# Part norms summed before their ones-product, a projection block moved ahead of an attention block, 1/rms on token quarters, lo parts on GpSimd

## The chip, the cores and the metric

The kernel runs on one core of a Trainium2 chip. The metric is the device time of one execution in microseconds (us), as the median of several runs. Nothing but the kernel runs on the chip at that time.

## What is computed

One Hymba-style decoder block on 512 tokens of width 1024, all in f32. Cut to what matters here:

```python
mod = silu(c) @ ada_w + ada_b                     # shift, scale, gate, twice
h = modulate(rmsnorm(x, norm1_g), shift1, scale1)
q, k, v, cb, cc, cu = split(h @ w_in)             # 18 blocks of 128 columns
attn = sliding_window_attention(q, k, v, sinks)   # window 128, 8 heads of 64
conv = cb * short_conv(cc * cu, conv_w)           # causal, width 3
merged = concat(rmsnorm(attn, g_a), rmsnorm(conv, g_c))   # the part norms
x = x + gate1 * (merged @ w_out)
h2 = modulate(rmsnorm(x, norm2_g), shift2, scale2)        # the second norm
x = x + gate2 * peer(h2, wq, subkeys, u_tab, v_tab)       # 16384 experts, top 16 per head
```

## The kernel before

Activations lie transposed: 128 partitions of columns by 512 tokens, so a norm over columns is a sum over partitions, made on TensorE by a product with a matrix of ones. A weight block (`raw`, 128x1024) is loaded by an SP DMA into one of five buffers. `split` (L175 to L177) makes of it `hi` on ScalarE (ACT, L176) and `lo = raw - hi` on VectorE (DVE, L177), and `mm3` (L197) issues 24 matmuls for it: L200 hi by H, L201 hi by L, and L202 lo by H.

Ahead of the experts there is a front part of some 260 us, and the change lies there. After the first norm come the projection blocks (`proj`, L336; four of the 18 are made earlier), mixed with the attention. The string `PLAN` (L50) sets the order in which they are written: `C m part` is a projection block of the short convolution (`conv`, L437), where part 0 ends in a copy `cc` on ACT, part 1 in `hb` and `y` on DVE and part 2 in `convT` on DVE. `A n` is `attend1` (L373) for query block n: eight score products `sc`, their scaling `s` on DVE (L388), the maximum `m` (L391), its negative `nm` (L394), eight exponentials on ACT (L397), and a division on DVE (L405). `B n` is `attend2` (L408): each head's `s` is transposed on TensorE (`pT`, L416), copied out by ACT (L418) and multiplied with the values (`po`, L425). `M` is two columns' blocks of the modulation matrix (`junk`, L213, on DVE). `S` is the sum of squares of the convolution part (`ssc`), and `N` makes its normed parts `mH`, `mL` (`part_norm`, L463).

After the plan comes `ssa`, the sum of squares of the attention part (L518 to L520). `square` (L234) squares one 128x512 slice on ACT and issues a ones-product for it, so each part norm has four products. `rstd` (L239) takes the root on ACT and the reciprocal on DVE, on 128x512, where all 128 partitions hold the same row. Then come the output products `py` (`out_half`, L472): first the half that needs the convolution part, for four blocks, then the other half and the other blocks. The residual `xT` is squared block by block and summed on DVE, and two ones-products (L551, L552) give `ss2`. `spill` (L528) transposes `xT` back to token rows (`xt`), copies it out on ACT (`xn`, L535, three buffers) and stores it. `modulated` (L226) makes `f`, `fH`, `fL` of the second norm, which the queries (`pq`) and their scores (`psc`, L742) take, ACT's copies `qs` (L735) between them. Everything behind that (keys, sorting, dense experts, gathered rows) the change leaves alone.

A scheduler fixes each engine's order of instructions when the kernel is built; on the chip every engine works through its own in that order and waits on semaphores. PSUM has six rotating banks (`bank`) and two for accumulators (`psa`).

Of the kernel before, what the change touches and what calls it, by code (L numbers as in the profile page):

```python
# [7 lines left out]
F32 = mybir.dt.float32  # L8
# [10 lines left out]
P = 128  # L19
T = 512  # L20
# [26 lines left out]

PLAN = ("q0 q1 k P2 M r0 V R P3 r1 q2 C00 r2 q3 T C01 M r3 M C02 A0 C10 M C11 A1 M C12 B0 C20 M M M A2 C21 B1 A3 "  # L50
        "C30 M C22 C31 C32 S B2 N B3 M M M")

SM = {}
# [36 lines left out]
def body(tc, p):  # L90
# [13 lines left out]
    rt, rt_s = pool("rt", side="right")  # L104
    R2 = dict(tag="s2", bufs=3)
    tp, tp_s = pool("tp", side="right")
    T2 = dict(tag="t2", bufs=9)
    xp, xp_s = pool("xp", side="right")

    def bank(name):  # L110
# [10 lines left out]
    def S(n, i=None, w=1):  # L121
        a, b = SM[n]
        return sm[:, a:b] if i is None else sm[:, a + i:a + i + w]
# [48 lines left out]
            tc.add_manual_dep(ins.ins, mark.ins.name, mybir.DependencyInfo(  # L172
                mybir.DependencyClass.Sync, mybir.DependencyReason.DATA), reason="pace")

    def split(h, l, f):  # L175
        nc.scalar.activation(h, f, AF.Copy)  # L176
        nc.vector.tensor_sub(l, f, h.bitcast(F32))  # L177

    def load(src):
        raw = ld.tile([P, D], F32, tag="ld", bufs=LD, name="raw")  # L180
        nc.sync.dma_start(raw, src)
        return raw

    def parts(src):

        raw = load(src)
        h = hl.tile([P, D], F32R, tag="h", bufs=4, name="hi")
        l = hl.tile([P, D], F32R, tag="l", bufs=4, name="lo")
        split(h, l, raw)
        return h, l  # L190

    def weights_of(src):

        h, l = parts(src.rearrange("p a b -> p (a b)"))
        return (lambda k: h[:, k * P:(k + 1) * P]), (lambda k: l[:, k * P:(k + 1) * P])

    def mm3(ps, w, rh, rl, ks=range(DC), k0=0, k1=DC - 1):  # L197
# [36 lines left out]
    def square(ps, b, i, n, w=None):  # L234
        q = tmp("sq")
        nc.scalar.activation(q, b, AF.Square)
        nc.tensor.matmul(ps, ones if w is None else w, q, start=(i == 0), stop=(i == n - 1))

    def rstd(ps, n):  # L239
        r = tmp("rstd")  # L240
# [93 lines left out]
    attnT = a1.tile([P, 4, T], F32, name="attnT")  # L334

    def proj(b):  # L336
        w = weights_of(p["w_in"][b])
        ps = bank("pj")
        mm3(ps, w, hh, hlo)
        return ps  # L340
# [119 lines left out]
    vT = tmp("vT")  # L460
    nc.scalar.activation(vT, pj[5], AF.Copy)
    kg = S("kg")
    def part_norm(ss, src, g, o):  # L463
        r = rstd(ss, 512)
        for k in range(4):
            f = tmp("f")
            nc.vector.scalar_tensor_tensor(f, src[:, k, :], S(g, k), r, op0=OP.mult, op1=OP.mult)
            split(mH[:, o + k, :], mL[:, o + k, :], f)
# [12 lines left out]
    for step in PLAN.split():  # L481
        n = [int(x) for x in step[1:]]
        match step[0]:
            case "k":
                nk = qk1(pj[4], qk0(pj[4]), kg)
            case "q":
                nq[n[0]] = q0(pj[n[0]], n[0])
            case "P":
                pj[n[0]] = proj(n[0])
            case "V":  # L490
                pt = bank("vt")
                for c in range(NCH):
                    nc.tensor.transpose(pt[:, c * P:(c + 1) * P], vT[:, c * P:(c + 1) * P], ident)
                nc.scalar.activation(vN.rearrange("p a b -> p (a b)"), pt, AF.Copy)
            case "r":
                qk2(nq.pop(n[0]), qT[:, n[0], :])
            case "R":
                qk2(nk, kT)
            case "T":
                nc.scalar.activation(rq, ssq, AF.Sqrt, bias=eps64)  # L500
                nc.vector.reciprocal(rq, rq)
            case "A":
                sa[n[0]] = attend1(n[0])
            case "B":
                attend2(n[0], sa[n[0]])
            case "C":
                conv(*n)
            case "M":
                more_ada()
            case "S":  # L510
                ssc = bank("ssc")
                for k in range(4):
                    square(ssc, convT[:, k, :], k, 4)
            case "N":
                mH = a1.tile([P, DC, T], F32R, tag="hH", name="mH")
                mL = a1.tile([P, DC, T], F32R, tag="hL", name="mL")
                part_norm(ssc, convT, "cg", 0)
    ssa = bank("ssa")  # L518
    for k in range(4):
        square(ssa, attnT[:, k, :], k, 4)  # L520
    for b in range(HEAD):
        out_half(b, 0)
    part_norm(ssa, attnT, "ag", 4)
    ab = S("ada_b")
# [3 lines left out]
    def spill(half, when):  # L528
        for c in range(NCH):
            ps = bank("xt")  # L530
            for i in range(4):
                after(nc.tensor.transpose(ps[:, i * P:(i + 1) * P], xT[:, 4 * half + i, c * P:(c + 1) * P], ident),
                      when)
            xn = rt.tile([P, 512], F32, name="xn", **R2)
            nc.scalar.activation(xn, ps, AF.Copy)  # L535
            nc.sync.dma_start(x1s[c][:, half * 512:(half + 1) * 512], xn)

# [10 lines left out]
        if b < 6:  # L548
            more_ada(3)
    sq = squared(xT[:, 6, :], sq)  # L550
    nc.tensor.matmul(ss2, ones, sq, start=True, stop=False)  # L551
    end = nc.tensor.matmul(ss2, ones, squared(xT[:, 7, :]), start=False, stop=True)  # L552
    nc.vector.tensor_add(mod[:, 24:48], mod[:, 24:48], ab[:, 24:48])
    nc.vector.scalar_tensor_tensor(s2, mod[:, 32:40], 1.0, S("n2g"), op0=OP.add, op1=OP.mult)
    a1_s.close()
# [16 lines left out]
    hx, hx_s = pool("hx")  # L572
    fH = hx.tile([P, DC, T], F32R, name="fH")
    fL = hx.tile([P, DC, T], F32R, name="fL")
    r2 = rstd(ss2, D)
    spill(0, end)
    spill(1, end)
    early = [(weights_of(p["wq"][b]), bank("pq")) for b in range(EARLY)]
    fs = []
# [552 lines left out]
```

## Time and profile before

| what | value |
|---|---|
| median of 3 runs | 1447.48 us (1445.46 to 1451.26) |
| profiled execution, own time | 1445.51 us |
| its span, first to last instruction | 1443.6 us |
| mean granted TensorE clock | 0.989 |
| busy: PE, DVE, ACT, POOL | 1391.7, 1242.0, 616.1, 411.4 us |

PE is TensorE, ACT ScalarE, POOL GpSimd, SP the engine that issues loads. Lines named L... are lines of the kernel before. The granted clock is a share of 2.4 GHz.

### The profile page before, as it was taken

The page shows a single profiled execution, that of the slowest core. Times are in us where ns is not written, and L with a number is a line of the kernel's source. Part 1 is how long each engine was busy: PE and PEld are TensorE (multiplying, and loading weights), DVE is VectorE, ACT ScalarE, POOL GpSimd, SP SyncE. Part 2 cuts the span into 40 slices and gives each one's busy share as a digit, 9 for nine tenths or more (in the row PEclk, how much of TensorE's full clock was granted, in tenths as well). Part 3 has the DMA queues.
Part 4 walks back from the last instruction along what each step waited for, and adds up shares of the span by engine and source line. Part 5 has one row for each costly group of instructions (what it writes and reads, how often), then busy time and mean ns, then how long its engine had stood idle before and what let it go on. Part 6 is the DMA issues. An engine that isn't in the chain of part 4 may idle for free.

```text
span 1443.6 us, 21238 instructions
## 1 busy us (share of the span) xinstructions
PE 1391.7 (96%) x7696; PEld 1222.1 (85%) x7696; DVE 1242.0 (86%) x2267; ACT 616.1 (43%) x1041; POOL 411.4 (29%) x292
## 2 busy tenths in 40 slices
PE   6999998999897999999999999999999999999998
PEld 4776776788897999999888888889999999889997
DVE  7778978799989999998668888888789988898964
ACT  4534646423633555464433434343343324333431
POOL 0000000000032330511034444446545546565400
PEclk9999999999998999999999999999999999999999
DMA  8645535222496997898999999999999999999843
GB/s 282 226 164 166 202 124 188 82 85 89 151 305 200 382 377 280 327 384 325 364 332 362 409 395 378 396 357 380 355 362 394 388 357 343 363 343 393 319 146 131
DMA packets 134377, 418.80 MB, mean 290 GB/s; under 512 B 12801, under 2 KB 39553, under 8 KB 132737
## 3 DMA queue, kind: packets, MB, share of 16 engines
q1 hardware_dynamic: 92800, 266.45, 51.1%
q0 software_dynamic: 41472, 151.01, 27.7%
q8 instruction: 60, 0.98, 0.3%
q14 instruction: 45, 0.36, 0.1%
HBM read 375.77 MB, written 41.62 MB: 289 GB/s over the span
## 4 chain that ended last, share of the span: by engine, by line
PE 63%; DVE 24%; DMA 5%; issue 5%; ACT 2%; POOL 1%; SPq 0%; DVEq 0%; ACTq 0%; POOLq 0%
PE o L997 11%; PE o L996 11%; PE o L998 11%; PE pa L200 6%; PE pa L202 6%; PE pa L201 6%; DVE lo L177 4%; DVE junk L213 2%; DVE B L946 2%; DVE junk L784 1%; PE py L200 1%; PE py L201 1%; DVE I L636 1%; PE py L202 1%; POOL row L776 1%
## 5 line engine op out<-in xcount | busy, mean ns | idle before, releaser
L176 ACT ACTIVATE hi<-raw 128x1024 fp32r<-128x1024 f32 x298 | 312.2, 1054 | 308.2 <-PE pa L201 71.7
L177 DVE TENSOR_TENSOR lo<-raw,hi 128x1024 fp32r<-128x1024 f32 x298 | 363.2, 1221 | 42.4 <-ACT hi L176 42.0
L202 PE MATMUL pa<-h2H,lo 128*128 128x352 f32 x1024 | 330.5, 323 | 8.2 <-DVE lo L177 8.2
L200 PE MATMUL pa<-h2H,hi 128*128 128x352 f32 x1024 | 332.9, 325 | 1.4 <-ACT sp L624 1.4
L201 PE MATMUL pa<-h2L,hi 128*128 128x352 f32 x1024 | 329.5, 322 | 0.0
L997 PE MATMUL o<-lo,wwh 128*128 128x512 f32 x768 | 299.2, 390 | 0.9 <-DVE lo L177 0.9
L996 PE MATMUL o<-hi,wwh 128*128 128x512 f32 x768 | 299.6, 390 | 0.0
L998 PE MATMUL o<-hi,wwl 128*128 128x512 f32 x768 | 298.8, 389 | 0.0
L776 POOL DMA_INDIRECT row<-in_uR,eG x128 | 187.4, 1464 | 319.5 <-PE o L998 181.8
L776 POOL DMA_INDIRECT row<-in_vL,eG x128 | 179.8, 1405 | 135.4 <-PE o L998 68.6
L784 DVE SCALAR_TENSOR_TENSOR junk<-row,h2N 128x1024 bf16<-128x1024 f32 x128 | 154.2, 1224 | 63.0 <-DMA row<-in_uR,eG 62.8
L202 PEld LDWEIGHTS pa<-h2H,lo 128*128 128x128 f32 x1024 | 193.2, 189 | 9.4 <-DVE lo L177 9.4
L200 PEld LDWEIGHTS pa<-h2H,hi 128*128 128x128 f32 x1024 | 192.7, 188 | 3.7 <-ACT sp L624 1.5
L201 PEld LDWEIGHTS pa<-h2L,hi 128*128 128x128 f32 x1024 | 193.1, 189 | 2.2
L912 DVE SCALAR_TENSOR_TENSOR ga<-row,av,ga 128x1024 f32<-128x1024 f32 x127 | 163.1, 1284 | 29.7 <-DMA row<-in_vL,eG 22.0
L776 POOL DMA_INDIRECT row<-in_uR,eH x32 | 44.0, 1376 | 493.2 <-DVE eq L695 402.9
L998 PEld LDWEIGHTS o<-hi,wwl 128*128 128x128 f32 x768 | 144.2, 188 | 30.3
L997 PEld LDWEIGHTS o<-lo,wwh 128*128 128x128 f32 x768 | 144.2, 188 | 29.3 <-DVE lo L177 1.5
L996 PEld LDWEIGHTS o<-hi,wwh 128*128 128x128 f32 x768 | 144.1, 188 | 28.3 <-issue 0.2
L176 ACT ACTIVATE wwh<-w 128x768 fp32r<-128x768 f32 x64 | 54.2, 846 | 164.0 <-DVE w L979 118.0
L978 ACT ACTIVATE w<-G 128x32 f32<-128x32 f32 x128 | 22.3, 221 | 190.4 <-DVE wwl L177 179.9
L177 DVE TENSOR_TENSOR wwl<-w,wwh 128x768 fp32r<-128x768 f32 x64 | 61.1, 955 | 9.8 <-ACT wwh L176 9.8
(265 smaller groups left out, 1852.0 us busy)
## 6 DMA issues: line engine op xcount, KB each, us to landing
raw<-in_uL SPq DMA_DIRECT2D x128, 512.0 KB
raw<-in_vL SPq DMA_DIRECT2D x128, 512.0 KB
Gd<-st SPq DMA_DIRECT2D x12, 2048.0 KB
G<-Gd SPq DMA_DIRECT2D x16, 1536.0 KB
ada<-in_ada SPq DMA_DIRECT2D x32, 512.0 KB
Ad<-sp SPq DMA_DIRECT2D x34, 352.0 KB
sp<-Ad SPq DMA_DIRECT2D x34, 352.0 KB
raw<-in_w_in SPq DMA_DIRECT2D x18, 512.0 KB
```

The costliest lines, as they stand in the source:

```text
L176: nc.scalar.activation(h, f, AF.Copy)
L177: nc.vector.tensor_sub(l, f, h.bitcast(F32))
L200: nc.tensor.matmul(ps, wh(k), rh(k), start=(k == k0), stop=False)
L201: nc.tensor.matmul(ps, wh(k), rl(k), start=False, stop=False)
L202: mark[0] = nc.tensor.matmul(ps, wl(k), rh(k), start=False, stop=(k == k1))
L213: nc.vector.scalar_tensor_tensor(junk, raw, 1.0, cact, op0=OP.mult, op1=OP.mult, accum_out=mod[:, b:b + 1])
L776: d = nc.gpsimd.indirect_dma_start(out=t, out_offset=None, in_=tab, in_offset=bass.IndirectOffsetOnAxis(ap=e, axis=0))
L784: return nc.vector.scalar_tensor_tensor(junk, t, 1.0, h, op0=OP.mult, op1=OP.mult, accum_out=a)
L912: nc.vector.scalar_tensor_tensor(ga, t, av[:, k:k + 1], ga, op0=OP.mult, op1=OP.add)
L996: nc.tensor.matmul(o, wh[:, cs], vh[:, hs], start=(j == 0), stop=False)
L997: nc.tensor.matmul(o, wh[:, cs], vl[:, hs], start=False, stop=False)
L998: last = nc.tensor.matmul(o, wl[:, cs], vh[:, hs], start=False, stop=(j == NJ - 1))
```

## The change

1. In `PLAN`, `C20` (24 products) stands ahead of `B0`, not behind it.
2. The `lo` of the 14 projection blocks made by `proj` is computed on GpSimd; those of `w_out` and later weights stay on DVE.
3. A part norm squares its four slices on ACT, adds them (conv part: on GpSimd; attention part: on DVE), and issues one ones-product in place of four.
4. The first half block of `py` is written ahead of the attention part's sum.
5. In the second norm the sum over partitions is made by eight products that put the four token quarters on four groups of 32 partitions (`grouped`), so root and reciprocal work on 128x128 instead of 128x512 (`grouped_root`), and four products with columns of the identity spread the result over all partitions again, into PSUM (`spread`), between the two halves of `spill`. `xn` takes buffers of the pool that `tmp` uses, which has 13 instead of 9.

```diff
-        "A1 M C12 B0 C20 M M M A2 C21 ..."
+        "A1 M C12 C20 B0 M M M A2 C21 ..."
-    T2 = dict(tag="t2", bufs=9)
+    T2 = dict(tag="t2", bufs=13)
-    def split(h, l, f):
+    def split(h, l, f, by=nc.vector):
         nc.scalar.activation(h, f, AF.Copy)
-        nc.vector.tensor_sub(l, f, h.bitcast(F32))
+        by.tensor_sub(l, f, h.bitcast(F32))
...
+    def grouped(ps, q, first, last):
+        for c in range(NCH):
+            end = nc.tensor.matmul(ps[32 * c:32 * c + 32, 0:P], ones[:, 0:32], q[:, c * P:(c + 1) * P],
+                                   start=first, stop=last)
+        return end
+    def grouped_root(ps, n):
+        r = cp.tile([P, P], F32, tag="r", name="r", bufs=1)
+        nc.scalar.activation(r, ps[:, 0:P], AF.Sqrt, scale=1.0 / n, bias=eps)
+        nc.vector.reciprocal(r, r)
+        return r
+    def spread(r):
+        ps = psa.tile([P, 512], F32, tag="a", name="rr")
+        for c in range(NCH):
+            nc.tensor.matmul(ps[:, c * P:(c + 1) * P], ident[:, 32 * c:32 * c + 1].to_broadcast([P, P]), r,
+                             start=True, stop=True)
+        return ps
...
     def proj(b):
-        w = weights_of(p["w_in"][b])
+        w = weights_of(p["w_in"][b], nc.gpsimd)
...
+    def summed(src, by):
+        q = tmp("sq")
+        nc.scalar.activation(q, src[:, 0, :], AF.Square)
+        for k in range(1, 4):
+            q2 = tmp("sq")
+            nc.scalar.activation(q2, src[:, k, :], AF.Square)
+            by.tensor_add(q, q, q2)
+        ps = bank("ss")
+        nc.tensor.matmul(ps, ones, q, start=True, stop=True)
+        return ps
...
-                ssc = bank("ssc")
-                for k in range(4):
-                    square(ssc, convT[:, k, :], k, 4)
+                ssc = summed(convT, nc.gpsimd)
...
-    ssa = bank("ssa")
-    for k in range(4):
-        square(ssa, attnT[:, k, :], k, 4)
-    for b in range(HEAD):
+    out_half(0, 0)
+    ssa = summed(attnT, nc.vector)
+    for b in range(1, HEAD):
         out_half(b, 0)
...
-            xn = rt.tile([P, 512], F32, name="xn", **R2)
+            xn = tmp("xn")
...
-    nc.tensor.matmul(ss2, ones, sq, start=True, stop=False)
-    end = nc.tensor.matmul(ss2, ones, squared(xT[:, 7, :]), start=False, stop=True)
+    grouped(ss2, sq, True, False)
+    end = grouped(ss2, squared(xT[:, 7, :]), False, True)
...
-    r2 = rstd(ss2, D)
+    r2 = grouped_root(ss2, D)
     spill(0, end)
+    r2 = spread(r2)
     spill(1, end)
```

ACT's order from the exponentials of A0 to those of A2. The 128x128 forms belong to query block 0, the 128x256 forms to the later ones. Before (A0's exponentials, B0's copies, A1's exponentials, B1's copies, A2's exponentials):

```order
L397 ACT_TABLE_LOAD
L397 ACTIVATE s,den<-s,nm 128x128 x8
L401 ACTIVATE es__754<-es__754 128x8
L176 ACTIVATE hi<-raw 128x1024 x2
L418 ACTIVATE pT<-pT 128x128 x8
L434 ACTIVATE attnT<-po 128x4x128
L397 ACTIVATE s,den<-s,nm 128x256 x8
L401 ACTIVATE es__881<-es__881 128x8
L442 ACTIVATE cc<-pj 128x512
L176 ACTIVATE hi<-raw 128x1024 x2
L418 ACTIVATE pT<-pT 128x256 x8
```

After the change:

```order
L418 ACT_TABLE_LOAD
L418 ACTIVATE s,den<-s,nm 128x128 x8
L422 ACTIVATE es__754<-es__754 128x8
L463 ACTIVATE cc<-pj 128x512
L176 ACTIVATE hi<-raw 128x1024 x2
L418 ACTIVATE s,den<-s,nm 128x256 x8
L422 ACTIVATE es__881<-es__881 128x8
L463 ACTIVATE cc<-pj 128x512
L439 ACTIVATE pT<-pT 128x128 x4
```

A1's exponentials now stand ahead of B0's copies, and so does the second `cc`, which reads C20's products; B0's other four copies follow behind one more `hi`. (Line numbers of the changed file are 21 to 33 higher.)

PE's order at the two part norms. Before, the conv part's three first ones-products stand behind the last projection block, the fourth among B2's transposes, and the attention part's four behind B3's last products:

```order
L237 MATMUL ssc<-sq,ones 128x512 x3
L416 MATMUL pT<-cst,s 128x128 x7
L237 MATMUL ssc<-sq,ones 128x512
L416 MATMUL pT<-cst,s 128x128
...
L425 MATMUL po<-pT,vN 64x128 x8
L237 MATMUL ssa<-sq,ones 128x512 x4
L200 MATMUL py<-mH,hi 128x512
```

After the change:

```order
L493 MATMUL ss<-sq,ones 128x512
L437 MATMUL pT<-cst,s 128x128 x8
L446 MATMUL po<-pT,vN 64x128
...
L202 MATMUL py<-mH,lo 128x512
L493 MATMUL ss<-sq,ones 128x512
L200 MATMUL py<-mH,hi 128x512
```

Each sum is one product; the first stands ahead of all of B2's transposes, the second behind the twelve products of the first half block of `py`.

PE's order at the second norm. Before:

```order
L551 MATMUL ss_1652<-sq,ones 128x512
L552 MATMUL ss_1652<-sq,ones 128x512
L532 MATMUL xt<-cst,xT 128x128 x32
L200 MATMUL pq<-fH,hi 128x512
```

After:

```order
L242 MATMUL ss_1652<-sq,ones 32x128 x8
L562 MATMUL xt<-cst,xT 128x128 x16
L256 MATMUL rr<-r,cst 128x128 x4
L562 MATMUL xt<-cst,xT 128x128 x16
L200 MATMUL pq<-fH,hi 128x512
```

The four spreading products `rr` stand between the halves of the transposes. On ACT all eight `xn` now stand ahead of the first `fH`, where five did before.

## Rows read from the trace of the kernel before

**Rows 1.** Page: the chain that ended last, share of the span by engine

```profile
PE 63%; DVE 24%; DMA 5%; issue 5%; ACT 2%; POOL 1%; SPq 0%; DVEq 0%; ACTq 0%; POOLq 0%
```

**Rows 2.** Busy by stage: length, PE, PEld, DVE, ACT, POOL, PEclk, DMA share, GB/s

```profile
120.00:166.00 46.00, 45.56 (x238) 35.91 (x237) 41.88 (x93) 24.85 (x74) 0.00 (x0) 0.96 0.48 158
166.00:187.00 21.00, 18.15 (x113) 10.65 (x111) 18.41 (x25) 13.25 (x30) 0.00 (x0) 0.92 0.60 205
231.00:261.00 30.00, 23.29 (x111) 16.79 (x111) 16.82 (x22) 26.33 (x61) 0.00 (x0) 0.94 0.34 122
```

**Rows 3.** Page's groups: all lo parts: busy us, mean ns | idle before, releaser

```profile
L177 DVE TENSOR_TENSOR lo<-raw,hi 128x1024 fp32r<-128x1024 f32 x298 | 363.2, 1221 | 42.4 <-ACT hi L176 42.0
```

**Rows 4.** PE in order of time: start, us, instruction; first lo product, then B0 to B1

```profile
60.62 1.41 PE L202 MATMUL pj<-hH,lo 128*128 128x512 f32 x1
...
114.55 0.27 PE L416 MATMUL pT<-cst,s 128*128 128x128 f32 x1
...
121.79 0.80 PE L200 MATMUL pj<-hH,hi 128*128 128x512 f32 x1
...
128.48 2.00 PE L383 MATMUL sc<-kT,qT 64*128 64x256 f32 x16
...
136.03 1.09 PE L416 MATMUL pT<-cst,s 128*128 128x128 f32 x8
...
140.38 1.31 PE L425 MATMUL po<-pT,vN 128*64 128x128 f32 x16
```

**Rows 5.** ACT in order of time, 101 to 146: exponentials of A0, A1, A2

```profile
103.01 1.28 ACT L397 ACT_TABLE_LOAD   x1
...
106.62 0.40 ACT L397 ACTIVATE s<-s,nm 128x128 f32<-128x128 f32 x1 [2.33 <-DVE nm L394]
...
123.31 0.51 ACT L397 ACTIVATE s<-s,nm 128x256 f32<-128x256 f32 x1 [0.81 <-DVE hb L445]
...
127.27 0.19 ACT L401 ACTIVATE es__881<-es__881 128x8 f32<-128x8 f32 x1
...
144.47 0.51 ACT L397 ACTIVATE s<-s,nm 128x256 f32<-128x256 f32 x1 [2.15 <-DVE nm L394]
```

**Rows 6.** DVE in order of time, 106 to 124: from A0's maximum to A1's

```profile
106.42 0.17 DVE L394 TENSOR_SCALAR nm<-m 128x8 f32<-128x8 f32 x1
...
109.58 0.69 DVE L446 TENSOR_TENSOR hb<-pj,cc 128x512 f32<-128x512 f32 x1
...
117.95 1.22 DVE L213 SCALAR_TENSOR_TENSOR junk<-ada,cact 128x1024 bf16<-128x1024 f32 x1
...
123.11 0.17 DVE L394 TENSOR_SCALAR nm<-m 128x8 f32<-128x8 f32 x1
```

**Rows 7.** PE in order of time at the two part norms

```profile
165.44 2.74 PE L237 MATMUL ssc<-sq,ones 128*128 128x512 f32 x6
...
170.46 0.27 PE L416 MATMUL pT<-cst,s 128*128 128x128 f32 x1
...
182.09 5.34 PE L237 MATMUL ssa<-sq,ones 128*128 128x512 f32 x8 [2.24 <-ACT sq L236]
186.86 0.79 PE L200 MATMUL py<-mH,hi 128*128 128x512 f32 x1
```

**Rows 8.** DVE and ACT in order of time at the part norms (two views)

```profile
184.05 0.69 DVE L177 TENSOR_TENSOR mL<-f,mH 128x512 fp32r<-128x512 f32 x1
...
168.82 0.63 ACT L236 ACTIVATE sq<-convT 128x512 f32<-128x512 f32 x1 [2.35 <-DVE convT L452]
```

**Rows 9.** PE, DVE and ACT in order of time at the second norm (three views)

```profile
240.13 0.79 PE L200 MATMUL pq<-fH,hi 128*128 128x512 f32 x1 [3.00 <-ACT fH L230]
...
259.13 1.16 PE L742 MATMUL psc<-sk,qs 128*128 128x128 f32 x8 [2.65 <-ACT qs L735]
...
234.39 3.35 DVE L242 RECIPROCAL rstd<-rstd 128x512 f32<-128x512 f32 x1 [1.22 <-ACT rstd L241]
...
238.25 1.21 ACT L535 ACTIVATE xn<-xt 128x512 f32<-128x512 f32 x2 [2.44 <-DMA x1s<-xn]
```

More of the change, by code (lines that the diff above doesn't have):

```diff
@@ L46 @@
 PACE = (1.75, 4.2)
-PLAN = ("q0 q1 k P2 M r0 V R P3 r1 q2 C00 r2 q3 T C01 M r3 M C02 A0 C10 M C11 A1 M C12 B0 C20 M M M A2 C21 B1 A3 "
+PLAN = ("q0 q1 k P2 M r0 V R P3 r1 q2 C00 r2 q3 T C01 M r3 M C02 A0 C10 M C11 A1 M C12 C20 B0 M M M A2 C21 B1 A3 "
         "C30 M C22 C31 C32 S B2 N B3 M M M")
@@ L182, in load, with parts @@
         return raw
-    def parts(src):
+    def parts(src, by=nc.vector):
         raw = load(src)
@@ L188, in parts, with weights_of @@
         l = hl.tile([P, D], F32R, tag="l", bufs=4, name="lo")
-        split(h, l, raw)
+        split(h, l, raw, by)
         return h, l
-    def weights_of(src):
-        h, l = parts(src.rearrange("p a b -> p (a b)"))
+    def weights_of(src, by=nc.vector):
+        h, l = parts(src.rearrange("p a b -> p (a b)"), by)
         return (lambda k: h[:, k * P:(k + 1) * P]), (lambda k: l[:, k * P:(k + 1) * P])
@@ L237, in square @@
         nc.tensor.matmul(ps, ones if w is None else w, q, start=(i == 0), stop=(i == n - 1))
+    def grouped(ps, q, first, last):
+        for c in range(NCH):
+            end = nc.tensor.matmul(ps[32 * c:32 * c + 32, 0:P], ones[:, 0:32], q[:, c * P:(c + 1) * P], start=first,
+                                   stop=last)
+        return end
[10 more added lines that the diff above has]
+        return ps
     def rstd(ps, n):
```

## The prediction

> **What bounds the kernel now.** I read the page's chain first: 63% of the span is PE's own work [rows 1], so in most of the kernel only less PE work or less PE waiting helps. The reader then goes to the table by stage, because the change touches only the front part, from about 60 to 260 us. Between 120 and 166 us PE is idle for 0.44 us, between 166 and 187 it has 2.85, and between 231 and 261 it has 6.7, at a granted clock of 0.94 there, so part of that stretch ran at 1.2 instead of 2.4 GHz [rows 2]. All that waiting is not much above 10 us, with some 4 us more in B0 (below). From the queries on, the order of all engines is as before, so what is won or lost by 260 us should reach the end as it is. The views in order of time of PE, ACT and DVE then show, for each place, which wait ends last.
>
> About 0.5%, 7.2 us, is what a measurement of this kernel can tell from no change; I use it as the border below.
>
> **Part 1, the lo parts on GpSimd.** On DVE a lo takes 1.22 us [rows 3]. GpSimd did nothing in this stretch [rows 2], so its price is unknown: DVE's 1.22 us is the lower bound, three times that, 3.7 us, my upper bound. Even at the upper bound it is shorter than the block of 24 products, 5.5 us at PE's full pace, so GpSimd keeps up, and with four buffers for lo the later ones have over ten us to spare. Only the first has no lead: its products start at 60.62 [rows 4] with the lo just ready, and would start 0 to 1.6 us later (a lo that starts at 58.5 and takes 1.2 to 3.7 us). I take +0.3, near the lower end, since PE has a rotation product to do until 60.6.
>
> The Trainium skill, GPSIMD Engine Reference, section 3.1, gives 1.96 times DVE's time for an f32 operation with two inputs. An estimate by that page is 2.4 us for a lo, and this term would be 0.4. No run here shows it.
>
> **Part 2, C20 ahead of B0.** B0 begins at 114.55 and C20 at 121.79, so B0 holds PE for 7.24 us; B1, with twice the transposes and products, holds it from 136.0 to 141.6 [rows 4], so B0's work is 2.8 us and the other 4.4 are waits. C20 itself then takes 6.7 us instead of 5.5, because its first products run at the lower clock level (the first lasts 0.80) [rows 4]. If C20 filled the wait, 4.4 + 1.2 = 5.6 us would be won. But in the new order ACT has A1's exponentials and one `cc` ahead of B0's copies. I follow that chain. (Durations of ACT's small steps that have no row here are the distances at which they follow each other in its view in order of time: `cc` 0.49, `hi` 0.97, a copy of B0 0.21, a copy of B1 0.27.)
> - A0's exponentials started at 106.62, behind `nm` at 106.42 [rows 5, 6]. Three lo go from DVE ahead of that `nm`, 3.7 us, but the table load ends only at 104.3 [rows 5], so they start about 104.3, and last 3.2 us to 107.5. The `cc` behind them takes 0.5, so `hb` starts at 108.0, where it started at 109.58.
> - From `hb` to A1's `nm` DVE was busy throughout, for 13.5 us [rows 6]. The same work less one `junk` (1.15) is 12.4, so `nm` of A1 comes at 120.4.
> - A1's exponentials took 4.1 us (123.31 to 127.4) [rows 5], so they end at 124.6; `cc` 0.5; four copies 0.8; one `hi` 1.0; four copies 0.8; the last products 0.7: 128.4.
>
> The scores of A2 come next. They started at 128.48 [rows 4] and would now start at 128.4. So PE has C20 done at 120.0 and then waits for 5 us: the wait of B0 is moved behind C20, not removed. I take 0 for this part. The ends are -1.5 (if the table load, too, comes earlier) and +2.5 (if one lo on GpSimd stands in DVE's way on this chain).
>
> **Part 3, what the same queue does to B1.** The last two copies of B1 now stand behind A2's exponentials on ACT, and PE has only the scores of A3 and two products to do until then. Those were done at 144.0. If A2's exponentials start when they did, at 144.47 [rows 5], the copies come after 148.6 and the products at 149.1: +5.1. If A2's chain is earlier by what A1's is (2.7) and by the two lo that stood on DVE behind A1's `nm` (2.4), they start at 139.4 and nothing is lost. A2's chain starts with its scores, and those are not earlier, so I don't take the lower end; but DVE is freer. I take a third, +1.7.
>
> **Part 4, the conv part's sum.** Before, four products (8 records, about 3.4 us), seven transposes between them (0.9) and a wait (0.6) filled 165.44 to 170.46 [rows 7]. Now one product of 0.86 us stands ahead of all transposes, behind `convT` (0.7), a `hi` or a square (1.0 and 0.6, [rows 8] for the square), and an addition on GpSimd (0.6, if as fast as DVE's 128x512 operations, to 1.8): it ends near 169.1, and seven transposes later it is 170.0, -0.4. If DVE comes to the last `convT` later, since w_out's lo are still on DVE, it is up to +2.5; the lower end is -0.9. I take +0.3. So three products and the wait are taken out, and the wait for the sum takes their place.
>
> **Part 5, the attention part's sum.** B3 ends at 179.85; then PE waits 2.24 us and makes four products until 186.86 [rows 7]. A block's first half is 12 products, 2.7 us, so the second block started at 189.6. Now the first block comes up, but its last three products need the fourth `mL`, which came at 184.05 to 184.7 [rows 8]. The squares' additions on DVE stand behind that `mL` and a `junk`: 184.7 + 1.15 + three of 0.6 = 187.7; the one product ends at 188.6, and the second block starts there: -1.0. The ends: -3.3 (sum ready when the first block is done) and +0.7 (one more `junk` ahead). The halves that need the attention part follow 8.2 us later, at 196.8, and their `mL` come from 194.7 on, so no new wait there. I take -1.0.
>
> **Part 6, the second norm.** PE waited 3.0 us for the first `fH` and 2.65 for `qs`, with a reciprocal of 3.35 us and a wait of 2.44 on `xn` buffers ahead [rows 9]. The reciprocal on a quarter is about 0.9. `rr` costs PE 1.05 (four products of the kind that `psc` has, [rows 9], 1.16 with the last one's end). `xT`'s second 16 transposes end at about 237.9 and the last `xn` at 238.6, then `fH`: the first `pq` at 239.4 instead of 240.13, -0.7. ACT, which sets the rest up to `qs`, then has three `xn` (1.5) fewer to do behind that `fH`: `qs` and `psc` -2.2. Ends: -0.5 (only the first gain) and -2.65 (the whole wait of `psc`). I take -1.9, as the copies that read `f` may be mixed less well.
>
> **The sum.** 0.3 + 0 + 1.7 + 0.3 - 1.0 - 1.9 = -0.6 us. Against the profiled execution (1445.51 us, span 1443.6) that is 1444.9. The median of the runs is 2 us above it, and the prediction goes by the median: 1447.48 - 0.6 = **1446.9 us**. The sums of the ends are -8.3 and +11.9.
>
> **Rival A, faster: C20 fills the wait.** If A1's exponentials end by 120, B0 runs without a stall behind C20. That takes A1's `nm` by 116, 4.4 us earlier than my chain gives; DVE has three lo fewer ahead of A0's `nm` and may do the `junk` in other gaps. Then part 2 is -5.6 and part 3 is 0: -0.6 - 5.6 - 1.7 = -7.9, **1439.6 us**, down to 1437 with the second norm and the attention sum at their lower ends. Against it: `hb` is tied to `cc`, and `cc` to A0's exponentials and the table load, and neither moves by more than 2.3 us.
>
> **Rival B, slower: GpSimd and DVE stand in each other's way.** The forecast takes the lo off DVE for nothing. If DVE must instead stop while GpSimd works on a lo, A1's and A2's chains, on which B0 and B1 hang one for one, each get two lo back, at GpSimd's length. At twice DVE's 1.22 us [rows 3] that is 4 x 2.44 = 9.8 us: **1456.7 us**. It decides from a lo of 1.8 us on (4 x 1.8 = 7.2). For it: DVE is busy for 41.88 of the 46 us from 120 on [rows 2], and `junk`, `y` and lo all read two tiles. Against it: the `junk` can be put off, and only operations that are caught are delayed; no row of before shows GpSimd at work there.
>
> The Trainium skill, SBUF — State Buffer, section "Who interferes with whom", says that GpSimd's only port pair is DVE's second one, held as an exclusive lock, and that a DVE instruction with two SBUF inputs contends with a GpSimd instruction that reads SBUF. By that rule rival B is what happens to `junk`, `y` and the remaining lo, while the scaling of scores, which reads PSUM and one SBUF tile, goes on. The trace before can't show it.
>
> **How the numbers follow.** The forecast, within 7.2 us either way, gets 0.58: its terms are small and of both signs. Rival A gets 0.23 and rival B 0.19. So: faster by over 0.5% 0.23, within 0.5% 0.58, slower by over 0.5% 0.19. The range reaches from the lower end of rival A, 1437, to just beyond rival B's price, 1458, which leaves out about 1 in 10 on either side, and takes in all but the last tenth or so of the sums of the ends.
>
> **What would show it.** In the profile after: `nm` of A1 at about 120 and PE idle for 4 to 5 us behind C20 (part 2); one wait on ACT's `pT` copies ahead of B1's last products (part 3); one 128x512 product at about 168 with a wait on GpSimd ahead (part 4); the second `py` block at 188 to 189 relative to before's time (part 5); a 128x128 reciprocal of 0.9 us and the first `psc` some 2 us earlier in its stage (part 6); the lo on GpSimd at 1.2 to 3.7 us, and `junk` at its old length, 1.22 [rows 6]. The prediction is wrong if B0 runs without a wait behind C20, if `junk` or `y` last longer while GpSimd works, or if the stage behind 260 us changes its length.

## The result and the profile after

| | before | after |
|---|---|---|
| median of 9 runs | 1447.48 us | 1454.56 us |
| lowest to highest | 1442.37 to 1451.87 | 1449.63 to 1457.44 |
| profiled execution, its span | 1445.51, 1443.6 | 1454.56, 1452.0 |

The ratio is 1.0053 with a 95% interval of 1.0034 to 1.0073: slower by 5 to 10.6 us. That is inside the range, but the forecast was -0.6 us, and the time went the other way.

Where in the span it is lost shows in six places on PE, read from its view in order of time: start of the transposes of v (`vt`, ahead of which nothing that matters was changed but the first lo), start of A2's scores, end of the last projection product, end of B3's products, end of the last `py`, start of the first `psc`. Counted from `vt` on, an early or late first load drops out. Times in us:

| stretch | before | after | difference | prediction's part |
|---|---|---|---|---|
| `vt` to A2's scores | 61.5 | 66.2 | +4.7 | 2: 0 |
| A2's scores to the last projection product | 37.1 | 44.3 | +7.2 | 3: +1.7 |
| to the end of B3 | 14.2 | 16.2 | +2.0 | 4: +0.3 |
| to the end of `py` | 51.1 | 51.5 | +0.4 | 5: -1.0 |
| to the first `psc` | 28.1 | 25.9 | -2.2 | 6: -1.9 |
| sum | 192.2 | 204.1 | +11.9 | |

Behind the first `psc` the pair of profiled executions shows 4 us less in the changed kernel: the kernel before waits 2.6 us for lo parts on DVE between 900 and 1300 us, the one after not at all. The change doesn't touch that stretch. Its orders on PE, DVE, ACT and GpSimd are the same in all 16 profiled executions of this document, and its length still varies from 1180.5 to 1188.4 us. So the 11.9 us say where PE loses time, and the median says how much: 7.1 us in all.

The table by stage of the kernel after, columns as in [rows 2]:

```profile
120.00:166.00 46.00, 35.24 (x180) 25.75 (x179) 35.56 (x74) 20.36 (x71) 5.27 (x2) 0.81 0.39 129
166.00:187.00 21.00, 17.56 (x83) 13.29 (x81) 18.20 (x28) 10.22 (x19) 4.55 (x3) 0.92 0.54 178
231.00:261.00 30.00, 26.22 (x143) 20.07 (x141) 25.57 (x40) 18.18 (x37) 0.00 (x0) 1.00 0.65 218
```

From 120 to 166 us PE is busy for 35.2 us instead of 45.6, and the granted clock is 0.81 instead of 0.96. This is the place. Only the stage of the second norm is better, 1.00 against 0.94.

PE around B0 and B1, in order of time:

```profile
121.49 0.60 PE L437 MATMUL pT<-cst,s 128*128 128x128 f32 x4
129.93 0.85 PE L446 MATMUL po<-pT,vN 128*64 128x128 f32 x4 [7.84 <-ACT pT L439]
...
133.69 2.36 PE L404 MATMUL sc<-kT,qT 64*128 64x256 f32 x16
141.56 1.03 PE L437 MATMUL pT<-cst,s 128*128 128x128 f32 x8
143.86 0.40 PE L446 MATMUL po<-pT,vN 128*64 128x128 f32 x2 [1.26 <-ACT pT L439]
...
150.91 1.50 PE L404 MATMUL sc<-kT,qT 64*128 64x256 f32 x4 [1.66 <-DVE s L409]
153.50 1.12 PE L446 MATMUL po<-pT,vN 128*64 128x128 f32 x8
```

C20 does run in the time in which B0 waited before [rows 4], and then PE waits 7.84 us at one go for the copies of B0. The granted clock is at its lower level from 124.2 to 134.5 us, so A2's scores (2.00 us before, 2.36 now) already run partly at it. B1 itself, A3's scores and the first two products of the next block took 8.0 us before (136.0 to 144.0); now they end with B1's last products at 154.6, 13.0 us after B1's first transpose. The other 94 products of the blocks behind it take 23.4 us, 1.9 more than before, with the lower clock level from 151.5 to 158.4 us in them.

ACT at the same time, where the queue order of the prediction can be seen:

```profile
125.10 0.51 ACT L418 ACTIVATE s<-s,nm 128x256 f32<-128x256 f32 x1 [7.97 <-DVE nm L415]
...
129.62 0.74 ACT L439 ACTIVATE pT<-pT 128x128 f32<-128x128 f32 x4
...
147.97 0.51 ACT L418 ACTIVATE s<-s,nm 128x256 f32<-128x256 f32 x1 [1.85 <-DVE nm L415]
...
152.01 0.63 ACT L439 ACTIVATE pT<-pT 128x256 f32<-128x256 f32 x2
```

ACT stands idle for 7.97 us because its next instruction is A1's exponential and DVE has no `nm` yet, while the four transposes that it could copy are done at 122.1. The copies follow behind the exponentials, at 129.62. The same happens at 147.97: B1's last two copies wait behind A2's exponentials until 152.01.

DVE and, below it, GpSimd (POOL) in order of time:

```profile
106.45 0.17 DVE L415 TENSOR_SCALAR nm<-m 128x8 f32<-128x8 f32 x1
...
110.45 0.69 DVE L467 TENSOR_TENSOR hb<-pj,cc 128x512 f32<-128x512 f32 x1 [0.31 <-ACT cc L463]
...
111.58 3.79 DVE L426 TENSOR_SCALAR s<-s,den 128x128 f32<-128x128 f32 x8
...
124.91 0.15 DVE L415 TENSOR_SCALAR nm<-m 128x8 f32<-128x8 f32 x1
...
129.71 4.29 DVE L426 TENSOR_SCALAR s<-s,den 128x256 f32<-128x256 f32 x8
```

```profile
111.45 2.46 POOL L177 TENSOR_TENSOR lo<-raw,hi 128x1024 fp32r<-128x1024 f32 x1 [5.06 <-ACT hi L176]
...
131.39 2.46 POOL L177 TENSOR_TENSOR lo<-raw,hi 128x1024 fp32r<-128x1024 f32 x1 [11.77 <-ACT hi L176]
...
174.55 3.19 POOL L491 TENSOR_TENSOR sq<-sq 128x512 f32<-128x512 f32 x2 [29.02 <-ACT sq L490]
179.89 1.45 POOL L491 TENSOR_TENSOR sq<-sq 128x512 f32<-128x512 f32 x1 [2.15 <-ACT sq L490]
```

The same divisions before the change:

```profile
113.64 1.65 DVE L405 TENSOR_SCALAR s<-s,den 128x128 f32<-128x128 f32 x8
...
131.36 2.18 DVE L405 TENSOR_SCALAR s<-s,den 128x256 f32<-128x256 f32 x8
```

The eight divisions of A0 (multiplications of a tile by a column, 1/`den`) take 3.79 us, where they took 1.65, those of A1 4.29, where they took 2.18, each time with a lo on GpSimd in them. The one that starts at 111.58 alone lasts 2.42 us and ends when that lo ends, at 113.9.

PE at the part norms, and PE, DVE and ACT at the second norm:

```profile
181.38 1.25 PE L493 MATMUL ss<-sq,ones 128*128 128x512 f32 x2 [3.44 <-POOL sq L491]
...
202.09 1.42 PE L493 MATMUL ss<-sq,ones 128*128 128x512 f32 x2 [2.71 <-DVE sq L491]
```

```profile
253.56 0.49 PE L200 MATMUL pq<-fH,hi 128*128 128x512 f32 x1 [1.45 <-ACT fH L230]
...
271.56 1.16 PE L773 MATMUL psc<-sk,qs 128*128 128x128 f32 x8 [1.87 <-ACT qs L766]
...
248.05 0.95 DVE L249 RECIPROCAL r<-r 128x128 f32<-128x128 f32 x1 [0.22 <-ACT r L248]
...
250.84 2.06 ACT L565 ACTIVATE xn<-xt 128x512 f32<-128x512 f32 x4 [0.57 <-PE xt L562]
```

Both sums are now waited for, 3.44 and 2.71 us (the attention part's 2.24 before, [rows 7]); in the second norm the waits of [rows 9] fall from 3.00 and 2.65 to 1.45 and 1.87.

### The profile page after: what moved, and what is told of

It reads as the page before. It is cut to its first block, busy times and chain, and to the rows that moved or that the text cites. A ratio compares the mean times of both kernels' runs of the same rounds, so it can differ in the third digit from the quotient of the medians.

```text
span 1452.0 us, 21288 instructions
## 1 busy us (share of the span) xinstructions
PE 1391.5 (96%) x7704; PEld 1222.4 (84%) x7704; DVE 1242.5 (86%) x2256; ACT 616.4 (42%) x1041; POOL 456.4 (31%) x309
## 4 chain that ended last, share of the span: by engine, by line
PE 55%; DVE 17%; issue 8%; DMA 6%; POOL 4%; ACT 2%; POOLq 0%; SPq 0%; DVEq 0%; ACTq 0%
PE pa L202 7%; PE pa L200 7%; PE pa L201 7%; PE o L1029 7%; PE o L1027 7%; PE o L1028 6%; DMA row<-in_uR,eG 4%; POOL row L807 4%; DVE lo L177 3%; DVE junk L815 2%; PE pq L200 2%; DVE B L977 2%; PE pq L202 2%; PE pq L201 2%; PE py L200 1%
## 5 line engine op out<-in xcount | busy, mean ns | idle before, releaser
L177 DVE TENSOR_TENSOR lo<-raw,hi 128x1024 fp32r<-128x1024 f32 x284 | 345.4, 1218 | 36.5 <-ACT hi L176 36.1
L807 POOL DMA_INDIRECT row<-in_uR,eG x128 | 195.6, 1528 | 311.4 <-PE o L1029 172.7
L807 POOL DMA_INDIRECT row<-in_vL,eG x128 | 176.6, 1380 | 137.0 <-PE o L1029 68.5
L177 DVE TENSOR_TENSOR wwl<-w,wwh 128x768 fp32r<-128x768 f32 x64 | 60.9, 952 | 10.8 <-ACT wwh L176 10.8
```

Source lines behind the costliest of these rows:

```text
L177: by.tensor_sub(l, f, h.bitcast(F32))
L807: d = nc.gpsimd.indirect_dma_start(out=t, out_offset=None, in_=tab, in_offset=bass.IndirectOffsetOnAxis(ap=e, axis=0))
```

## The experiments

Three suspects: the order on ACT that C20's new place brings (order theory), the lo on GpSimd in DVE's way (port theory), and the conv part's sum. All runs are compared with runs of the kernel before on the same chip. The stretches are those of the table above, as differences to before, each from one profiled execution. The first one is 58.9 to 63.2 us in the seven executions whose orders there are those of before (61.5 in before's own), so single values of it are good to some 2 us.

| run | ratio, 95% interval | to A2 | to last pj | to B3 | to `py` | to `psc` |
|---|---|---|---|---|---|---|
| lo_on_dve | 1.0063, 1.0040 to 1.0085 | +3.9 | +1.8 | +3.2 | +1.0 | -2.2 |
| b0_first | 1.0060, 1.0040 to 1.0079 | +0.3 | +1.0 | +9.4 | 0.0 | -2.2 |
| only_lo | 1.0008, 0.9991 to 1.0025 | +0.3 | +1.0 | +2.1 | -0.8 | -0.5 |
| only_plan | 1.0008, 0.9992 to 1.0024 | +3.9 | +0.2 | +1.4 | -0.8 | -0.3 |
| only_sums | 1.0072, 1.0048 to 1.0095 | -0.6 | 0.0 | +8.4 | -1.5 | -0.4 |
| conv_sum_dve | 1.0025, 1.0006 to 1.0044 | -2.6 | +0.9 | +5.3 | -0.6 | +0.3 |
| attn_norm2 | 0.9983, 0.9968 to 0.9999 | +1.7 | +0.1 | 0.0 | +1.4 | -2.0 |
| only_norm2 | 0.9987, 0.9971 to 1.0003 | -0.3 | 0.0 | 0.0 | -0.7 | -2.2 |
| four_products | 1.0008, 0.9989 to 1.0028 | +1.8 | +1.0 | +2.2 | -1.0 | -2.0 |
| spare_lo | 1.0127, 1.0096 to 1.0157 | +15.9 | +3.5 | -0.8 | +0.1 | +2.4 |
| sum_late_norm2 | 1.0017, 0.9998 to 1.0037 | -0.1 | +0.3 | -1.7 | +3.6 | -2.2 |
| sum_late_attn | 1.0007, 0.9987 to 1.0028 | 0.0 | 0.0 | -1.7 | +3.1 | -2.2 |
| plan_and_lo | 1.0067, 1.0045 to 1.0090 | +4.7 | +4.5 | +0.1 | -2.5 | -0.3 |
| no_conv_sum | 1.0061, 1.0040 to 1.0082 | +4.7 | +4.5 | +0.1 | +0.2 | -2.0 |

### One part undone, or one alone

lo_on_dve:

```diff
-        w = weights_of(p["w_in"][b], nc.gpsimd)
+        w = weights_of(p["w_in"][b])
```

> The changed kernel, with the projection's lo parts back on DVE. After the change the first psc started 12.4 us later than before (271.56 against 259.13), of which 9.2 us came up by the end of B1. Order theory (ACT's queue has A1's exponentials ahead of B0's copies, and A2's ahead of B1's last): that order is mostly kept here, so PE still waits over 5 us for the copies of B0, the first psc is 6 to 12 us later than in the kernel before, and the time is 4 to 8 us above before. Port theory (GpSimd's lo stop DVE on the chains of A0 and A1): the eight divisions of A0 and A1 return from 3.8 and 4.3 us to 1.7 and 2.2, the wait of B0 falls under 3 us, and the time is within 2 us of before.

b0_first:

```diff
-        "... C12 C20 B0 M M M A2 ..."
+        "... C12 B0 C20 M M M A2 ..."
```

> The changed kernel with B0 ahead of C20 again; the lo stay on GpSimd. Order theory: B0's copies stand ahead of A1's exponentials on ACT again, the one wait of 7.8 us goes, the scores of A2 start within 2 us of before's 128.5, and the first psc is within 2 us of before's 259.1; time -2 to +2 us against before. Port theory: DVE's divisions and y still take up to 2 us longer whenever a lo runs on GpSimd, the scores of A2 start 4 us or more late, and the time is 4 to 8 us above before.

only_lo is the kernel before with the first of these two lines the other way round (and `split`'s new argument), only_plan the kernel before with the second.

> The kernel before with nothing but the projection's lo parts on GpSimd. Port theory: some DVE operations (divisions, y, junk) last up to 2.4 us longer while GpSimd works on a lo, and what DVE saves by 14 lo of 1.22 us is given back: 3 to 8 us above before. Order theory: such stretches show, but DVE has enough slack in the old order; -2 to +2 us.

> The kernel before with nothing but C20 ahead of B0. Order theory: PE waits 4 to 8 us for B0's copies behind C20, and the granted clock falls to its lower level behind that; the scores of A2 start 2 to 5 us later than before, B1's last products wait too if A2's exponentials stand ahead of their copies; +3 to +7 us. Port theory: GpSimd does nothing here, so C20 fills B0's wait: -5 to 0 us.

Neither theory came out whole. With the lo back on DVE, the divisions are back at 1.66 and 2.19 us, as the port theory had it, but PE still waits 7.1 us for B0's copies, as the order theory had it, and the time stays at +0.63%, 9.1 us, a little above its 4 to 8. What the lo added in the changed kernel is in the stretch behind A2's scores, +1.8 without it instead of +7.2. With B0 first, that wait is gone and A2's scores come 0.3 us late, as expected; yet the time stays at +0.60%, because the stretch to the end of B3, which I had not suspected, grew to 23.6 us. PE's waits there, of b0_first:

```profile
PE ss L493 <- POOL sq L491: 9.0, 1, 9.0
```

And each of the two alone costs nothing that can be measured. In only_plan the wait is there,

```profile
131.04 0.85 PE L425 MATMUL po<-pT,vN 128*64 128x128 f32 x4 [7.57 <-ACT pT L418]
```

but it takes the place of B0's old waits (4.4 us) and of C20's slow start (1.2), so less is lost than waited for. Its stretches are from the slowest of its twelve executions (1455.56 us, median 1447.26). The 3.9 us to A2's scores are not peculiar to that one, though: lo_on_dve, with the same orders up to there, has 3.9, too. Why the median shows so little of them (+1.2 us, at most +3.5 by the interval) stays open. The +3 to +7 us that I expected of it were too many; so were the 3 to 8 of only_lo by the port theory.

### The conv part's sum

only_sums is the kernel before with `summed` for both part norms and the first half block of `py` moved, conv_sum_dve with `summed` for the conv part alone, its additions on DVE:

```diff
-                ssc = bank("ssc")
-                for k in range(4):
-                    square(ssc, convT[:, k, :], k, 4)
+                ssc = summed(convT, nc.vector)
```

> The kernel before with nothing but the two part norms' sums as changed (conv part added on GpSimd, one product ahead of B2's transposes; attention part added on DVE behind the first half block of py). GpSimd theory: the last projection product to the last product of B3, 14.3 us before, takes 19 to 24, since the additions on GpSimd and DVE's divisions of A3 stop each other and the last convT comes late; with the rest, +5 to +9 us. Theory that only the queue order of C20 and the lo do harm: that stretch stays within 2 us of before, time -2 to +2.

> The kernel before with nothing but the conv part's sum as one product, its additions on DVE. If GpSimd is what makes the sum late: the stretch from the last projection product to the end of B3 is at most 2 us longer than before's 14.3, time 0 to +2. If the place of the one product is what costs (it waits for the last convT with all transposes behind it, where before seven of eight went ahead of the fourth product): 3 to 6 us longer, time +3 to +6, and a wait of 4 us or more ahead of that product.

only_sums hits in the stretch, 22.6 us to the end of B3; its +0.72%, 10.4 us, is a little above the 9 that I expected at most. GpSimd and, below it, DVE in that run, in order of time:

```profile
164.76 2.68 POOL L470 TENSOR_TENSOR sq<-sq 128x512 f32<-128x512 f32 x2 [164.31 <-ACT sq L469]
171.84 2.58 POOL L470 TENSOR_TENSOR sq<-sq 128x512 f32<-128x512 f32 x1 [4.40 <-ACT sq L469]
```

```profile
164.35 4.29 DVE L405 TENSOR_SCALAR s<-s,den 128x256 f32<-128x256 f32 x8
...
170.36 0.68 DVE L452 TENSOR_TENSOR convT<-pj,y 128x512 f32<-128x512 f32 x1
```

The two first additions hold up DVE's divisions (4.29 instead of 2.18), so the last `convT` ends at 171.0, where it ended at 168.8 before; then a lo and a `junk` on DVE hold up the third addition, which takes 2.58 us (1.45 in the changed kernel). PE waits 8.7 us. In conv_sum_dve, with no GpSimd, it still waits:

```profile
PE ss L472 <- DVE sq L470: 5.2, 1, 5.2
```

So of the 8.4 us that the sum costs, 5.3 come without GpSimd, from the place of the one product with its additions on DVE: all transposes of B2 stand behind it, where seven had gone ahead of the fourth product [rows 7]. Some 3 are GpSimd. In time conv_sum_dve is +0.25%. (sum_late_norm2, below, has the same additions on DVE and the product behind B2, and the loss in this stretch is gone: it is the place.)

four_products is b0_first with `square`'s four products for the conv part again:

```diff
-                ssc = summed(convT, nc.gpsimd)
+                ssc = bank("ssc")
+                for k in range(4):
+                    square(ssc, convT[:, k, :], k, 4)
```

> The changed kernel with B0 ahead of C20 and with the conv part's four ones-products again (no additions on GpSimd); the lo stay on GpSimd, the attention sum and the second norm as changed. Theory that the conv part's sum was what was left of the loss in b0_first (23.6 us from the last projection product to the end of B3, 14.2 before): that stretch falls to 17 us or less, and the time is within 3 us of before (against +8.7 for b0_first). If instead the lo on GpSimd cost the rest: the stretch stays above 20 us and the time 5 us or more above before.

It hits: 16.4 us to the end of B3, and +0.08%. With C20 behind B0 and without the one sum, the lo on GpSimd, the attention sum and the second norm together change nothing that can be measured. b0_first and four_products differ in that sum alone: it is 7.2 us there.

### Which of the two carries the changed kernel

plan_and_lo is the kernel before with two parts of the change; no_conv_sum is the changed kernel with the last edit above (four products), nothing else undone.

```diff
-        "... C12 B0 C20 M M M A2 ..."
+        "... C12 C20 B0 M M M A2 ..."
-        w = weights_of(p["w_in"][b])
+        w = weights_of(p["w_in"][b], nc.gpsimd)
```

> The kernel before with C20 ahead of B0 and the projection's lo on GpSimd, nothing else. Each alone cost 0.08%. Together they give the order of ACT in which A2's exponentials stand ahead of B1's last two copies, as in the changed kernel. If the two act on each other: PE waits 6 us or more for B0's copies and 3 us or more for the scores of A3 and B1's last products together; from the scores of A2 to the last projection product 43 to 45 us (37.1 before), the first psc 9 to 12 us later, time +5 to +9. If they only add up: 38 to 39 us, time +1 to +4.

> The changed kernel with the conv part's four ones-products again and nothing else undone. If what the plan and the lo cost together is the same loss in another place (DVE has caught up by then, so the conv part's sum costs only 2 us in the changed kernel): the time stays 4 to 8 us above before. If the conv part's sum is the whole of it: within 2 us of before, as four_products was.

PE's waits in plan_and_lo between 100 and 160 us:

```profile
PE po L425 <- ACT pT L418: 8.2, 2, 7.8
PE sc L383 <- DVE s L388: 1.5, 1, 1.5
```

0.08% and 0.08% alone, 0.67% together: in time they act on each other. ACT's order is the changed kernel's, with B1's last two copies behind A2's exponentials; in only_plan and lo_on_dve all eight copies stand ahead of them. The stretch behind A2's scores is 41.6 us, short of the 43 to 45 I expected but more than the 38 to 39 of parts that add up. Of its +4.5 us, 2.8 are at B1: from its first transpose to its last products it takes 10.8 us, where it was 8.0 before. The other 1.7 lie in A2's scores and the block between them and B1, at a granted clock of 0.80 against 0.96 in only_plan; lo_on_dve has 0.79 there, and its +1.8 us, without any lo on GpSimd. Two more of my expectations missed: B1's and A3's waits together are 1.9 us and not 3 or more, and the first `psc` comes 6.5 us later and not 9 to 12. Summed over the whole front part, the profiled executions just add up (4.4 and 2.1 us alone, 6.5 together). That the two act on each other rests on the medians, on ACT's order and on the 2.8 us at B1.

And no_conv_sum stays at +0.61%, 8.8 us where I expected 4 to 8: in the changed kernel the conv part's sum carries nothing that the time shows. There the stretch to the end of B3 costs 2.0 us in the place of 8 to 9, since DVE is less late by the time PE comes to it: the last `convT` ends 1.1 us behind the last projection product, 3.2 before the change and 5.3 in only_sums. (In the profiled execution the stretch before that is 2.7 us shorter than in the changed kernel, too; the median doesn't show either.)

### The cost of GpSimd by itself

spare_lo is the kernel before, with a second lo on GpSimd that nobody reads:

```diff
         split(h, l, raw)
+        if twice[0]:
+            spare = a1.tile([P, D], F32, tag="spare", bufs=1, name="spare")
+            nc.gpsimd.tensor_sub(spare, raw, h.bitcast(F32))
```

> The kernel before, and besides: GpSimd computes the lo of the 14 projection blocks a second time, into a tile that nobody reads; DVE's own lo and every order stay. The doubled cost alone. Port theory: while one of these 14 (2.4 us each) runs, a DVE instruction with two SBUF operands (lo, junk, y) or a division (a copy-like form with one operand) waits for it and lasts up to 2.4 us longer, the scaling of scores, hb, convT (one operand in PSUM) and the maximum keep their 0.48, 0.69 and 2.28; the first psc comes 3 to 8 us later, time +2 to +7. Against it: all DVE operations keep their lengths; 0 us.

DVE and, below it, GpSimd in spare_lo:

```profile
109.56 3.42 DVE L177 TENSOR_TENSOR lo<-raw,hi 128x1024 fp32r<-128x1024 f32 x1
...
121.10 2.58 DVE L455 TENSOR_SCALAR y<-hb,sm 128x512 f32<-128x512 f32 x1
...
123.60 0.47 DVE L395 SCALAR_TENSOR_TENSOR s<-sc,rq,cs 128x256 f32<-128x256 f32 x1
...
124.00 1.91 DVE L409 TENSOR_TENSOR den<-den,es__764 128x8 f32<-128x8 f32 x1
```

```profile
109.50 2.41 POOL L194 TENSOR_TENSOR spare<-raw,hi 128x1024 f32<-128x1024 f32 x1 [3.86 <-ACT hi L176]
...
120.95 4.92 POOL L194 TENSOR_TENSOR spare<-raw,hi 128x1024 f32<-128x1024 f32 x2 [9.05 <-ACT hi L176]
```

The kind of operand is as expected, the size isn't: +18 us, more than twice the upper end, with the first `psc` 21 us later. A lo of DVE that meets one of GpSimd lasts 3.42 us instead of 1.22, `y` 2.58 instead of 0.48, and an addition of 128x8 elements 1.91 instead of 0.17. The scaling of scores, which reads PSUM and one tile of SBUF, keeps its 0.47 in the middle of it. The second lo also holds `raw` and `hi` until GpSimd is done, so loads come later, too. No wait of PE between `vt` and A2's scores, where 15.9 us are lost, ends with a load: the two long ones, 6.4 and 6.1 us, end with `qn` and `s` on DVE. How much of these goes back to loads the run can't say.

The Trainium skill, SBUF — State Buffer, section "Who interferes with whom", states this rule (GpSimd's port pair is DVE's second one, locked for a whole instruction, and an operation with two SBUF inputs or in a two-port mode contends). The traces agree: operations with two SBUF inputs and one-input multiplications that started while a lo ran on GpSimd were longer by about what that lo had left (`y` 2.58 us, above), those that read PSUM kept their length, and so did the maximum over a tile (2.29 while a lo ran, 2.28 otherwise, in the changed kernel). Whether the multiplications were in a two-port mode no trace shows. The Trainium skill, GPSIMD Engine Reference, section 3.1, gives 1.96 times DVE's time; here it is 2.40 to 1.22 us, 1.97.

### Towards a better version

attn_norm2 is the kernel before with the attention sum and the second norm of the change, only_norm2 with the second norm alone:

```diff
-    r2 = rstd(ss2, D)
+    r2 = grouped_root(ss2, D)
     spill(0, end)
+    r2 = spread(r2)
```

sum_late_norm2 has besides the second norm the conv part's sum as one product with additions on DVE, and behind B2; sum_late_attn has the attention sum as well:

```diff
-        "C30 M C22 C31 C32 S B2 N B3 M M M"
+        "C30 M C22 C31 C32 B2 S N B3 M M M"
```

> The kernel before with the attention part's sum and the second norm as changed, and with the plan, the lo and the conv part's sum as before: nothing runs on GpSimd, C20 stands behind B0. By all theories it wins what the second norm wins (2.1 us from the last py to the first psc in the changed kernel) and what the attention sum wins (-1 to 0): -3 to -1 us against before, and the best of all versions.

> The kernel before with nothing but the second norm as changed. From the last py product to the first psc 28.1 us before; 25.9 to 26.5 here; all else in the front part as before. Time -2.5 to -1 us, which the interval may not tell from 0.

> The kernel before with the second norm as changed, and the conv part's sum as one product with its additions on DVE, but S written behind B2 (C32 B2 S N B3), so that no transpose waits for it. If the place of the product is what cost 5 us in conv_sum_dve: the wait ahead of it is gone or under 1 us, the stretch from the last projection product to the end of B3 is 12 to 14 us (14.2 before), and the time -5 to -2 us against before, the best so far. If the additions on DVE cost: the stretch stays at 16 us or more.

> The same with the attention part's sum as changed, too (first half block of py ahead of it, additions on DVE). If that part saves three products (2.6 us) on PE: from the end of B3 to the last py at most 50 us (51.1 before) and 1 to 2 us faster than the version without it. If the product waits for DVE as it did in the changed kernel (2.7 us): equal or up to 2 us slower than the version without it.

The second norm's gain is there in each run, 2.0 to 2.2 us to the first `psc`; in time it is -0.13%, which the interval doesn't tell from 0. attn_norm2 (1444.25 us, ratio 0.9983) can't be told from only_norm2 (1443.92 us, 0.9987); that its interval just leaves out 1 is little evidence, as it is the lowest of 14 ratios. The attention sum itself won nothing in the stretch to the end of `py` (+1.4 against -0.7 without it).

sum_late_norm2 missed. The wait ahead of the one product is gone and the stretch to the end of B3 is 12.5 us, as expected, but the time isn't lower. Its waits:

```profile
PE ssa L237 <- ACT sq L236: 5.2, 1, 5.2
```

What was won ahead of it is waited for at the attention part's sum (2.2 us before, 5.2 now), which can't be made before B3's output is squared. sum_late_attn missed as well: from the end of B3 to the last `py` it takes 54.2 us where I expected at most 50, and its time (1.0007) can't be told from that of sum_late_norm2. There PE waits 2.6 us for the sum and 3.1 for `mH` and `mL`. Fewer ones-products only give PE less to do at a place where it waits for ACT and DVE anyway.

## Why the prediction was wrong

- **Part 1** (first lo, +0.3): right in size. `vt` comes 0.5 us later in the span.
- **Part 2** (0) failed by 4.7 us (single values are good to some 2), in its step "the same work less one `junk` is 12.4, so `nm` of A1 comes at 120.4". It came at 124.9. Half of that is `hb`: `nm` of A0 was not earlier at all (106.45 after, 106.42 before), since in the lo's place on DVE came `junk`s that waited for their loads (0.3 and 0.7 us) and the small maximum of two 128x8 tiles (L413) that waited for GpSimd (0.84 instead of 0.16), so `hb` started at 110.45 and not at 108.0. The other half is in the divisions, 3.79 instead of 1.65 us. The mechanism (the copies behind A1's exponentials) was right; the chain was too short, because it took the lo off DVE for nothing. I had listed one lo in DVE's way as the upper end, +2.5, and left it out of the sum. But the lo on GpSimd don't make the wait: `nm` of A1 comes 57.4 us behind `vt` in all six runs that have them there (the changed kernel's is one), 55.8 to 57.4 us in nine that have them on DVE, and PE waits over 7 us in lo_on_dve, too. Taking the lo off DVE won nothing for this chain, and that is the gain of 2.7 us that I had reckoned with.
- **Part 3** (+1.7) failed by 5.5 us, the largest miss. The end that I put at +5.1 came: B1's last products ended 13.0 us after B1's first transpose, against 8.0. `nm` of A2 came 14.1 us after its scores began, against 15.8 before; 5 us less would have been needed. I had argued that DVE is freer, but it lost 2.1 us in A1's divisions alone. Left out altogether was the lower clock behind such waits: the 94 products that follow took 1.9 us longer, and A2's scores and the block behind them 0.3.
- **Part 4** (+0.3) came to +2.0 in the changed kernel. By itself it was mis-sized by far more: 8.4 us in only_sums. The step that failed is "it ends near 169.1" for the one product, 3.5 us behind the last projection product. In conv_sum_dve, with no GpSimd, it only starts 5.2 us behind it: a lo stands on DVE ahead of the last addition, and the product and the eight transposes then run at the lower clock. And I reckoned 0.6 to 1.8 us for the addition on GpSimd and nothing for what it does to DVE, some 3 us more. The changed kernel hides this, as B1 has already made PE late.
- **Part 5** (-1.0) came to +0.4. The wait for the sum was in the reckoning, and the second block did start early: 8.5 us after the end of B3, within the 188 to 189 of the prediction (10.2 before). What failed is the assumption that this block keeps its pace: behind the wait it ran at the lower clock, 4.8 us for its 12 products instead of 2.7. One of them after the change and one before:

```profile
203.73 0.63 PE L201 MATMUL py<-mL,hi 128*128 128x512 f32 x1
190.49 0.39 PE L202 MATMUL py<-mH,lo 128*128 128x512 f32 x1
```

- **Part 6** (-1.9) was right, -2.2.
- **Rival B**, to which I gave 0.19, came in part: GpSimd at twice DVE's length, and DVE stopping for it on the chains of A0 and A1. The sign that I had named came, too: one `y` lasted 2.29 us instead of 0.75. That its time (1456.7) is near the 1454.56 is luck. Its price was four whole lo, 9.8 us; the traces show two stops of 2.1 us in the divisions. This alone costs nothing measurable (only_lo), and without it the loss stays (lo_on_dve, 1.0063): it needs the queue order of part 2 to reach PE, and where that pair is undone the conv part's sum, which I held to be worth 0.3, costs as much.

## What to carry to other kernels

Moving elementwise work from a busy VectorE to GpSimd takes it off VectorE only where VectorE's own operations meanwhile are of a kind that kept its length here (with an operand in PSUM, or a maximum over a tile); price a moved operation at what it stops, and look at which chain is running then. When a block is pulled forward to fill a wait, look at what comes ahead of the waiter on the third engine: here ACT sat idle for 8 us with copies behind an exponential that wasn't ready. And undo parts in pairs as well as singly: here two parts that cost nothing measurable alone made a loss together, a third made as much without them, the losses did not add up, and each single undoing left one of them.

## What was not expected of the hardware

A VectorE addition of 128x8 elements lasted 1.91 and 2.25 us in spare_lo instead of 0.17 because it met a GpSimd instruction; a lo of 1.22 us became 3.42, so what is added depends on what the GpSimd instruction has left and not on the length of the stopped one. It goes both ways: GpSimd's third addition took 2.58 us in only_sums instead of 1.45 when it met a lo and a `junk` of VectorE.
